# Two-layer mixer and expert-choice MoE on one core: the planner's costs of each step, and a step between engines

## The chip, the core and the metric

One core of a Trainium2 chip. The metric is the device time of one execution in microseconds (us), the median over runs. The core's engines run beside each other, each through its own queue of instructions in order: PE (TensorE, matmuls), DVE (VectorE), ACT (ScalarE), POOL (GpSimd), and SP, whose queue issues the DMA transfers. They wait for one another through semaphores.

## The reference

Two layers work on 256 latent tokens and 256 context tokens of 1024 channels, all in float32. In short:

```python
for l in range(DEPTH):                                   # 2 layers
    u = modulate(rms_norm(h), mod[0], mod[1])            # mod = silu(c) @ ada_w[l] + ada_b[l], six parts
    z = u @ w_in[l]                                      # one projection for four mixers and their gates
    ys = diff_attention(z), hyena(z), conformer(z), latent_attention(z)
    acc = sum(sigmoid(gate[i]) * (ys[i] @ w_branch[l][part i]) for i in range(4))
    h = h + mod[2] * (acc @ w_out[l])
    u = modulate(rms_norm(h), mod[3], mod[4])
    aff = softmax(u @ w_router[l])                       # 16 experts, each takes its top tokens
    h = h + mod[5] * scatter(gate * (silu(hg) * hu) @ w_exp_out[l])   # hg, hu = u[idx] @ w_exp_in[l]
return rms_norm(h)
```

In layer 1 only the latent tokens are finished. The expert weights are the bulk of the bytes: 16 experts of 12 MB in each of the two layers.

## The kernel before

Matmuls are done in three passes (`mm3`, L351): each operand is cut into a high and a low part (`split`, L346: ACT casts the high part at L348, DVE subtracts at L349), and L355, L356 and L357 are the three products. A weight piece of the input projection thus passes DMA (`wi`, L857), ACT, DVE (both into `wq`) and PE (`pm`). PSUM tiles come from small rings: `pm` has 2, `psc` 3, `px` 1, `pt` some.

The program is made of generators: the input projection (`stream`, L832), which feeds the gates (`tg`, L972), hyena, the conformer (`ca` taps on DVE at L1218, its norm at L1230 to L1250), two attentions (scores L1547, maxima L1260 and L1262, exponentials on ACT L1264, transposes L1270, products L1524, the differential norm L1533 to L1536, its end L1505 to L1510), `branch` (L986), which multiplies a mixer's output by a part of `w_branch` (cast to `wbrh` and `wbrl`) and adds the gated result to `acc` (L1042 to L1047), and the output projection (the end of `body`, L956 to L963): a unit of 24 matmuls, then `yo` on DVE (L960), the residual add on POOL (L961), and after it the transposes of `h` (L1742). The generator `products` (L466) makes the modulation vectors on DVE: for each 256 KB `aw` load (L283) a pair of multiplications with a running sum (L510, `aj` and `aw`), 192 instructions in layer 0; when a group is complete, four small instructions follow (L525, L526, L413, L414). The generator `loader` (L1633) issues the loads of expert weights: large `we` of 1 MB (L1678), small ones of 256 KB (L1676), as buffers come free, and the loads of `x` into `h` (L1593). Then the experts run (`experts`, L1936).

What sets the order is a planner, `Order` (L145). It holds a model clock for each engine and one for DMA (`load`: 2.95 us per MB). A generator yields either an event to wait for, a time, or a dictionary of costs by engine; `run` picks the first generator, in order of place, whose time has come on the model's PE clock, lets it emit its instructions, and books the costs: each engine of the dictionary starts when it is free and the engine ahead of it in the dictionary is done. The time that comes out is the earliest for the generator's next step. Since every engine runs its instructions in the order in which they were emitted, the costs set nothing but that order. `_a`, `_d` and `_q` are the costs of an instruction of n columns on ACT, DVE and POOL. Tuned numbers beside them (rings, leads, lags such as `PACE` in `products`) stay.

Of the kernel before, what the change touches and what calls it, by code (L numbers as in the profile page):

```python
# [144 lines left out]
class Order:  # L145
# [29 lines left out]
    def run(self, gens):  # L175

        live = [[g, self.first.pop(g, 0.0), None, None, self.wait.get(i, 0.0)] for i, g in enumerate(gens)]
        place = [i + self.place.get(i, 0) for i in range(len(gens))]
        live = [live[i] for i in sorted(range(len(gens)), key=lambda i: place[i])]
        while live:  # L180
            best = None
            for th in live:
                if th[2] is not None:
                    if th[2].t is None:
                        continue
                    th[1], th[2] = max(th[1], th[2].t), None
                if th[1] - th[4] <= self.t["pe"]:
                    best = th
                    break
                if best is None or th[1] - th[4] < best[1] - best[4]:  # L190
                    best = th
            assert best is not None, [th[0].__name__ for th in live]
            self.t["pe"] = max(self.t["pe"], best[1])
            try:
                y = best[0].send(best[3])
            except StopIteration:
                live.remove(best)
                continue
            best[3] = None
            if isinstance(y, Ev):  # L200
                best[2] = y
            elif isinstance(y, dict):
                e = self.t["pe"]
                for k, c in y.items():
                    k = k.strip()
                    if k == "pe" and e < self.cold:
                        c *= 2
                    e = self.t[k] = max(self.t[k], e) + c
                best[3] = e
            else:  # L210
                best[1] = y


def _a(n):
# [1 line left out]


def _d(n):
    return 0.07 + n / 960


def _q(n):
    return 0.1 + n / 480


@with_exitstack
def kernel(ctx: ExitStack, tc: tile.TileContext, x, ctxt, cols, skip, lamb, fng, ta, tb, tcn, td,
# [169 lines left out]
    def layer(l):  # L397
# [434 lines left out]
        def stream(items):  # L832
# [65 lines left out]
            def body():  # L898
                for j, (src, kind, units, fn, evs) in enumerate(items):
                    for s in range(2) if last else ((0,) if kind == "t" else (0, 1)):  # L900
                        if l == 0 or s == 1 or not last or (kind == "n" and units[0] == 0) or (kind == "t" and units[0] == 0):
                            yield us_ev[s]
                    if kind == "t":
                        t0, tn = units
                        for m in range(2):
                            yield p_ev[j, m]
                            wh, wl = parts[j, m]
                            if fn is gate_out:
                                yield from S.until(lambda: tg_n[0] < TGMAX)
                                tg_n[0] += 1  # L910
                            p = pm()

                            step = 256 if last else tn
                            for c in range(0, tn, step):
                                terms = [(wh[:, k, :], wl[:, k, :], u_at(0, k, t0 + c, step), u_at(1, k, t0 + c, step))
                                         for k in range(KC)]
                                for k in range(0, KC, PIECE[l]):
                                    if k == 4 and l == 0:
                                        yield us_ev[1]
                                    mm3(p[:, c:c + step], terms[k:k + PIECE[l]], first=k == 0, last=k == KC - PIECE[l])  # L920
                                    if c + step < tn or k < KC - PIECE[l]:
                                        yield {"pe": 3 * PIECE[l] * step * 0.00042}
                            done(j, m)
                            cost = fn(p[:, :tn], evs[m])
                            e = yield {"pe": 3 * PIECE[l] * step * 0.00042, **cost}
                            evs[m][0].t = e
                    else:
                        yield p_ev[j, 0]
                        yield p_ev[j, 1]
                        w = 160 if fn is kv_out else 256  # L930
                        for t in units:
                            pv = pm()[:, :w]
                            mm3(pv, [(u_at(0, k, t * 128, 128), u_at(1, k, t * 128, 128), parts[j, k // 4][0][:, k % 4, :w],
                                      parts[j, k // 4][1][:, k % 4, :w]) for k in range(KC)])
                            cost = fn(pv, evs, t)
                            e = yield {"pe": 24 * 0.00042 * w, **cost}
                        evs[0].t = e
                        done(j, 0, 1)

                drop(4)  # L940
                keep()
                gates_done.t = S.t["pe"]
                yield mods[l]["ev"][1]
                if l == 0:
                    yield res_ev
                for k in range(KC):
                    yield acc_ev[k]
                drop(len(accs))
                for q in range(4):
                    for i in range(2):  # L950
                        yield p_ev[jo + q, i]
                    w = [parts[jo + q, i] for i in range(2)]
                    c = slice(q % 2 * 256, q % 2 * 256 + 256)
                    for t in tchunks:
                        p = pm()[:, :256]
                        tt = slice(t * 128 - q0, (t + 1) * 128 - q0)  # L956
                        mm3(p, [(ac[k][0][:, tt], ac[k][1][:, tt], w[k // 4][0][:, k % 4, :], w[k // 4][1][:, k % 4, :])
                                for k in range(KC)])
                        o, hv = t2("yo", w=256), h[t][q // 2][:, c]
                        nc.vector.tensor_tensor(o, p, m2[t // 2][q // 2][:, c], op=OP.mult)  # L960
                        (nc.vector if q == 3 else nc.gpsimd).tensor_tensor(hv, hv, o, op=OP.add)  # L961
                        e = yield {"pe": 24 * 0.108, "dve": _d(256), "dve " if q == 3 else "pool": _d(256)}
                        h_ev[t, q].t = e  # L963
                    del w
                    done(jo + q, 0, 1)
# [20 lines left out]
        def branch(i, os, k0, ready, early):  # L986
# [34 lines left out]
            for d2 in range(4):  # L1021
# [5 lines left out]
                for m in range(2):  # L1027
# [6 lines left out]
                    g = tg.pop((i, kd))  # L1034
                    tg_n[0] -= 1
                    acc_n[kd] += 1
                    PE = {"pe": nk * 3 * TQ * 0.00042, "dve": _d(TQ)}
                    if acc_n[kd] == 1:
                        nc.vector.scalar_tensor_tensor(a, g, 1.0, p[:, :TQ], op0=OP.add, op1=OP.mult)
                        yield PE  # L1040
# [44 lines left out]
        def hyena():  # L1085
# [8 lines left out]
                tabs.append([c.rearrange("p (a f) -> p a f", a=2) for c in hl])  # L1094
                yield {"act": _a(512), "pool": _q(512)}
            cf, sf, ci, si = tabs
            MF = 12 * 0.213 * F

            def to_tokens(c0, name, parts):
                r = []  # L1100
# [1030 lines left out]
```

## Time and profile before

| | us |
|---|---|
| median of 3 runs | 2000.3 (1995.5 to 2003.9) |
| the profiled execution | 2003.7 |
| its span, first to last instruction | 2001.9 |
| PE busy | 1700.4 (85%) |
| DVE busy | 971.6 (49%) |
| ACT, POOL busy | 461.8 (23%), 217.3 (11%) |
| mean granted clock of PE | 0.913 |

The profile is of one execution. Its stages: layer 0's mixers from 0 to about 690 us, its experts to about 1150, layer 1's mixers to about 1535, its experts to the end. A row of a timeline gives the start, the duration, the engine, the line, the operation, output and inputs, the count, and in brackets how long the engine had been idle just before and what ended that. Buffer numbers are left out of names. The granted clock is a share of 2.4 GHz, the mean over the stretch.

### The profile page before, as it was taken

What the parts mean: (1) busy time and instruction counts of PE and PEld (TensorE: products, weight loads), DVE (VectorE), ACT (ScalarE), POOL (GpSimd) and SP (SyncE); (2) the same over time, 40 slices, a digit from 0 to 9 for tenths busy, and PEclk for the clock granted to TensorE, in tenths of its full rate; (3) what the DMA queues carried; (4) which work ended last, traced back from release to release, by engine and by line L of the source; (5) the groups of instructions that cost most, each with busy time, mean ns of one, the idle gap of its engine ahead of it and who ended that gap; (6) DMA issues with size and microseconds to landing.
All of it is one profiled execution on the core that took longest, in us unless ns stands there. A gap on an engine that the chain in (4) does not pass through costs nothing.

```text
span 2001.9 us, 27922 instructions
## 1 busy us (share of the span) xinstructions
PE 1700.4 (85%) x11128; PEld 1108.5 (55%) x11128; DVE 971.6 (49%) x2052; ACT 461.8 (23%) x933; POOL 217.3 (11%) x229
## 2 busy tenths in 40 slices
PE   5998999887999899899899788998988867666665
PEld 2677788665679634333333278888987423322222
DVE  4886789877764312212432285888864111111012
ACT  4423333323332100100110063344442000000000
POOL 1322011021201000000010042410211000000000
PEclk8999999888999899989999998999998877787777
DMA  7443334423345799999999954565759999999997
GB/s 280 168 140 112 127 116 134 147 90 95 99 134 225 250 365 411 418 418 416 415 415 416 401 177 146 165 200 163 227 185 357 414 414 414 413 413 412 414 413 284
DMA packets 204586, 550.72 MB, mean 275 GB/s; under 512 B 14054, under 2 KB 94120, under 8 KB 173992
## 3 DMA queue, kind: packets, MB, share of 16 engines
q1 hardware_dynamic: 204456, 548.94, 72.8%
q8 instruction: 88, 1.44, 0.3%
q14 instruction: 42, 0.34, 0.1%
HBM read 547.83 MB, written 1.05 MB: 274 GB/s over the span
## 4 chain that ended last, share of the span: by engine, by line
PE 48%; DMA 26%; DVE 14%; issue 6%; ACT 5%; POOL 1%; SPq 0%; ACTq 0%; DVEq 0%; POOLq 0%
DMA we<-in_w_ei_dram 14%; PE pm L1951 10%; DMA we<-in_w_eo_dram 7%; PE pm L355 7%; PE pm L357 6%; PE pm L356 6%; PE psc L1976 4%; DVE wq L349 3%; DMA h<-in_w_eo_dram 3%; PE psc L1840 2%; DVE aw L510 2%; PE psc L355 2%; ACT wq L348 1%; PE psc L357 1%; PE psc L356 1%
## 5 line engine op out<-in xcount | busy, mean ns | idle before, releaser
L1951 PE MATMUL pm<-we,xe 128*32 128x256 f32 (+1 forms) x2912 | 406.9, 542 | 96.3 <-DMA we<-in_w_ei_dram 94.4
L1951 PEld LDWEIGHTS pm<-we,xe 128*32 128x32 f32 (+1 forms) x2912 | 136.7, 136 | 343.3 <-issue 185.2
L355 PE MATMUL pm<-uh,wq 128*128 128x256 f32 (+1 forms) x832 | 293.4, 353 | 7.4 <-ACT wq L348 4.8
L356 PE MATMUL pm<-ul,wq 128*128 128x256 f32 (+1 forms) x832 | 283.7, 341 | 2.4 <-DVE ul L754 1.5
L357 PE MATMUL pm<-uh,wq 128*128 128x256 f32 (+1 forms) x832 | 283.2, 340 | 0.0
L1963 DVE SCALAR_TENSOR_TENSOR ea<-ea,pm 128x512 f32<-128x512 f32 (+1 forms) x32 | 17.7, 554 | 426.7 <-ACT ea L1962 426.7
L349 DVE TENSOR_TENSOR wq<-wi,wq 128x1024 fp32r<-128x1024 f32 x131 | 164.1, 1263 | 91.9 <-ACT wq L348 91.5
L1976 PE MATMUL psc<-we,eaT 128*32 128x256 f32 (+1 forms) x1280 | 170.9, 506 | 39.8 <-DMA we<-in_w_eo_dram 37.8
L355 PEld LDWEIGHTS pm<-uh,wq 128*128 128x128 f32 x832 | 161.9, 195 | 29.8 <-ACT wq L348 6.5
L356 PEld LDWEIGHTS pm<-ul,wq 128*128 128x128 f32 x832 | 162.2, 195 | 20.6 <-issue 3.9
L357 PEld LDWEIGHTS pm<-uh,wq 128*128 128x128 f32 x832 | 161.8, 194 | 16.8
L1988 DVE TENSOR_TENSOR ye<-psc,modr 32x512 f32<-32x512 f32 (+1 forms) x120 | 66.4, 553 | 204.8 <-PE psc L1976 203.4
L1976 PEld LDWEIGHTS psc<-we,eaT 128*32 128x32 f32 (+1 forms) x1280 | 58.3, 128 | 146.8 <-issue 74.8
L348 ACT CAST wq<-wi 128x1024 fp32r<-128x1024 f32 x132 | 136.1, 1043 | 10.7 <-DMA wi<-in_w_in_dram 9.3
L1962 ACT ACTIVATE ea<-pm 128x512 f32<-128x512 f32 (+1 forms) x32 | 15.7, 491 | 481.0 <-PE pm L1951 481.0
L1218 DVE SCALAR_TENSOR_TENSOR ca<-up,colt,ca 128x510 f32<-128x510 f32 (+29 forms) x120 | 80.8, 673 | 2.1
L355 PE MATMUL pm<-wq,uh 128*128 128x256 f32 (+1 forms) x240 | 72.7, 303 | 8.1 <-DVE rsq L319 4.0
L2020 ACT COPY eaT<-pt 128x512 f32<-128x512 f32 (+1 forms) x32 | 15.3, 479 | 278.2 <-PE pt L2018 278.2
L510 DVE SCALAR_TENSOR_TENSOR aw<-aw,h 128x512 f32<-128x512 f32 x96 | 77.1, 803 | 3.6
L1264 ACT ACTIVATE e<-psc,nm 128x512 f32<-128x512 f32 (+1 forms) x72 | 44.5, 618 | 146.8 <-DVE nm L1262 144.4
L356 PE MATMUL pm<-wq,uh 128*128 128x256 f32 (+1 forms) x240 | 70.7, 295 | 0.0
L357 PE MATMUL pm<-wq,ul 128*128 128x256 f32 (+1 forms) x240 | 70.7, 295 | 0.0
(407 smaller groups left out, 2639.0 us busy)
## 6 DMA issues: line engine op xcount, KB each, us to landing
we<-in_w_ei_dram SPq DMA_DIRECT2D x233, 1024.0 KB, 13.0
we<-in_w_eo_dram SPq DMA_DIRECT2D x110, 1024.0 KB, 14.6
wi<-in_w_in_dram SPq DMA_DIRECT2D x58, 1024.0 KB, 5.4
aw<-in_ada_t_dram SPq DMA_DIRECT2D x160, 256.0 KB, 5.3
we<-in_w_ei_dram SPq DMA_DIRECT2D x52, 256.0 KB, 9.0
wbr<-in_w_branch_dram SPq DMA_DIRECT2D x40, 256.0 KB, 5.6
h<-in_w_ei_dram SPq DMA_DIRECT2D x40, 256.0 KB, 16.2
h<-in_w_eo_dram SPq DMA_DIRECT2D x40, 256.0 KB, 16.2
```

Of the source, the lines that this page charges most:

```text
L348: nc.scalar.copy(hi, src)
L349: eng.tensor_tensor(lo, src, hi.bitcast(F32), op=OP.subtract)
L355: nc.tensor.matmul(out, lh, rh, start=first and i == 0, stop=False)
L356: nc.tensor.matmul(out, lh, rl, start=False, stop=False)
L357: nc.tensor.matmul(out, ll, rh, start=False, stop=last and i == n - 1)
L510: nc.vector.scalar_tensor_tensor(o, wt_, 1.0, cb[s, k], op0=OP.mult, op1=OP.mult, accum_out=ends[lm, g][0][:, s, c, k:k + 1])
L1218: nc.vector.scalar_tensor_tensor(o, up[:, :, max(d, 0):256 + min(d, 0)], cw[:, c0 + d:c0 + d + 1], o, op0=OP.mult, op1=OP.add)
L1264: nc.scalar.activation(e, p[:, :nk], AF.Exp, scale=scale, bias=nm, accum_out=s)
L1840: nc.tensor.matmul(p[:, kk * n:(kk + 1) * n], h[2 * s + b][k // 4][:, (k % 4) * 128:(k % 4 + 1) * 128], hot[:, 2 * i + b], start=b == 0, s ...
L1951: nc.tensor.matmul(dst[j * M:(j + 1) * M, :], lhs, w[o + j * FW // 512][:, j * FW % 512:j * FW % 512 + FW], start=k == 0, stop=k == KC - 1 ...
L1976: nc.tensor.matmul(py[j * M:(j + 1) * M, :FW], aT[:, c * 128 + q * M:c * 128 + (q + 1) * M], w[f % 2 * 2 + j * FW // 512][:, j * FW % 512: ...
L1988: nc.vector.tensor_tensor(ye[eg][s][c0 // 512][e4 * CAP:(e4 + 1) * CAP, c0 % 512:c0 % 512 + FW], py[r0:r0 + CAP, :FW], mod5[r0:r0 + CAP, c ...
```

## The change

Every engine's step in a dictionary is now followed by a step `HOP` of 0.1 us before the next engine of the same dictionary or the generator's next step may start. The costs of DVE and POOL get a larger fixed part and a larger slope (512 columns on DVE 0.603 to 0.690 us, on POOL 1.17 to 1.29); ACT's stay. A column of a matmul costs 0.000442 us in place of 0.00042 (a unit of 12 matmuls of 512 columns 2.58 to 2.72), a unit of the output projection 24 x 0.119 in place of 24 x 0.108. The number of instructions on PE, DVE, ACT and POOL, their operands and the bytes of the DMA transfers stay; some of the late expert loads go to other buffers. Line numbers of the changed kernel are 4 higher from L213 on.

```diff
@@ class Order, run: one generator's step is booked on the model's clocks
                     if k == "pe" and e < self.cold:
                         c *= 2
                     e = self.t[k] = max(self.t[k], e) + c
+                    e += HOP
                 best[3] = e
...
+HOP = 0.1
...
 def _d(n):
-    return 0.07 + n / 960
+    return 0.13 + n / 915

 def _q(n):
-    return 0.1 + n / 480
+    return 0.15 + n / 450
...
-                                        yield {"pe": 3 * PIECE[l] * step * 0.00042}
+                                        yield {"pe": 3 * PIECE[l] * step * 0.000442}
...
-                            e = yield {"pe": 24 * 0.00042 * w, **cost}
+                            e = yield {"pe": 24 * 0.000442 * w, **cost}
...
-                        e = yield {"pe": 24 * 0.108, "dve": _d(256), "dve " if q == 3 else "pool": _d(256)}
+                        e = yield {"pe": 24 * 0.119, "dve": _d(256), "dve " if q == 3 else "pool": _d(256)}
...
-                    PE = {"pe": nk * 3 * TQ * 0.00042, "dve": _d(TQ)}
+                    PE = {"pe": nk * 3 * TQ * 0.000442, "dve": _d(TQ)}
...
-            MF = 12 * 0.213 * F
+            MF = 12 * 0.226 * F
```

What it does to the order is shown at three places of layer 0. The first is the start of the output projection. On SP, with `wi` for its weights, `we` for the experts' and `aw` for the modulation products, before:

```order
L1593 DMA h_76<-in_x_dram 128x512
L995 DMA wbr<-in_w_branch_dram 128x2x256 x2
L857 DMA wi<-in_w_out_dram 128x8x256 x2
L1678 DMA we<-in_w_ei_dram 128x2048 x5
L1676 DMA we<-in_w_ei_dram 128x512 x4
L1678 DMA we<-in_w_ei_dram 128x2048 x2
L857 DMA wi<-in_w_out_dram 128x8x256
```

and changed:

```order
L287 DMA aw<-in_ada_t_dram 128x512 x3
L861 DMA wi<-in_w_out_dram 128x8x256
L287 DMA aw<-in_ada_t_dram 128x512
L1682 DMA we<-in_w_ei_dram 128x2048 x5
L1680 DMA we<-in_w_ei_dram 128x512 x4
L287 DMA aw<-in_ada_t_dram 128x512 x2
L1597 DMA h_74<-in_x_dram 128x512
L1597 DMA h_75<-in_x_dram 128x512
L1597 DMA h_76<-in_x_dram 128x512
L1682 DMA we<-in_w_ei_dram 128x2048 x2
L861 DMA wi<-in_w_out_dram 128x8x256
```

The `aw` loads and the three loads into `h` stood ahead of the expert loads and now stand among and behind them. On DVE at the same place, before (`acc` and `al` are the end of the gated sum, `yo` is the first work on the projection's results):

```order
L349 TENSOR_TENSOR wq<-wi,wq 128x1024
L1042 SCALAR_TENSOR_TENSOR tg<-tg,psc 128x512
L1047 TENSOR_TENSOR acc<-acc,tg 128x512
L1718 COPY cb_164<-psc 128x32
L349 TENSOR_TENSOR al<-acc,ah 128x512
L960 TENSOR_TENSOR yo<-pm,r_4716 128x256 x2
L1745 COPY hT<-pt 128x256
```

and changed, with one more pair of L514 just ahead of the first row:

```order
L514 SCALAR_TENSOR_TENSOR aj,ad<-aw,h_74 128x512
L514 SCALAR_TENSOR_TENSOR aw,ad<-aw,h_76 128x512
L514 SCALAR_TENSOR_TENSOR aj,ad<-aw,cb 128x512
L514 SCALAR_TENSOR_TENSOR aw,ad<-aw,h_75 128x512
L514 SCALAR_TENSOR_TENSOR aj,ad<-aw,h_74 128x512
L514 SCALAR_TENSOR_TENSOR aw,ad<-aw,h_76 128x512
L529 TENSOR_TENSOR as<-ad 128x32
L530 SCALAR_TENSOR_TENSOR modB_90<-as,colt 128x32
L417 TENSOR_SCALAR modA_89<-modB_90 128x16
L418 TENSOR_TENSOR modA_89<-modA_89,colt 128x16
L964 TENSOR_TENSOR yo<-pm,r_4718 128x256 x2
```

Four pairs of products and the four small instructions of their group now stand ahead of `yo`.

The second place is DVE ahead of the branch matmuls for which PE waits at 381 us. Before, from the split of the last weight piece to `wbrl`:

```order
L349 TENSOR_TENSOR wq<-wi,wq 128x1024
L510 SCALAR_TENSOR_TENSOR aj,ad<-aw,h_74 128x512
L510 SCALAR_TENSOR_TENSOR aw,ad<-aw,h_76 128x512
L1218 SCALAR_TENSOR_TENSOR ca<-up,colt,ca 128x2x243
L1218 SCALAR_TENSOR_TENSOR ca<-up,colt,ca 128x2x242
L1260 TENSOR_REDUCE mx<-psc 128x1
L1262 TENSOR_SCALAR nm<-mx 128x1
L1260 TENSOR_REDUCE mx<-psc 128x1
L1262 TENSOR_SCALAR nm<-mx 128x1
L349 TENSOR_TENSOR wbrl<-wbr,wbrh 128x512
```

and changed, from behind the split and one pair of taps on:

```order
L514 SCALAR_TENSOR_TENSOR aj,ad<-aw,cb 128x512
L514 SCALAR_TENSOR_TENSOR aw,ad<-aw,h_75 128x512
L1416 TENSOR_TENSOR ol<-px,oh 128x128
L1222 SCALAR_TENSOR_TENSOR ca<-up,colt,ca 128x2x244
L1222 SCALAR_TENSOR_TENSOR ca<-up,colt,ca 128x2x243
L514 SCALAR_TENSOR_TENSOR aj,ad<-aw,h_74 128x512
L514 SCALAR_TENSOR_TENSOR aw,ad<-aw,h_76 128x512
L1222 SCALAR_TENSOR_TENSOR ca<-up,colt,ca 128x2x243
L1222 SCALAR_TENSOR_TENSOR ca<-up,colt,ca 128x2x242
L1264 TENSOR_REDUCE mx<-psc 128x1
L1266 TENSOR_SCALAR nm<-mx 128x1
L514 SCALAR_TENSOR_TENSOR aj,ad<-aw,cb 128x512
```

After the last row come the second product of its pair, the second maximum and `wbrl`. Two more pairs of products and two more pairs of taps stand in the stretch, and one pair of products is between the maxima.

The third place is DVE ahead of the branch matmuls for which PE waits at 486 us. Before, from the split on:

```order
L349 TENSOR_TENSOR wq<-wi,wq 128x1024
L1493 RECIPROCAL re<-re 128x2
L1494 TENSOR_SCALAR e<-e,re,lamt 128x512
L1495 SCALAR_TENSOR_TENSOR e<-e,re 128x512
L1510 SCALAR_TENSOR_TENSOR ol<-pt,gsub_100,oh 128x128 x4
L1260 TENSOR_REDUCE mx<-psc 128x1
L1262 TENSOR_SCALAR nm<-mx 128x1
L510 SCALAR_TENSOR_TENSOR aj,ad<-aw,cb 128x512
L510 SCALAR_TENSOR_TENSOR aw,ad<-aw,h_75 128x512
L1260 TENSOR_REDUCE mx<-psc 128x1
L1262 TENSOR_SCALAR nm<-mx 128x1
L349 TENSOR_TENSOR wbrl<-wbr,wbrh 128x512
```

and changed, with a split of `wq` just ahead of the first row:

```order
L1497 RECIPROCAL re<-re 128x2
L1498 TENSOR_SCALAR e<-e,re,lamt 128x512
L1499 SCALAR_TENSOR_TENSOR e<-e,re 128x512
L514 SCALAR_TENSOR_TENSOR aj,ad<-aw,cb 128x512
L514 SCALAR_TENSOR_TENSOR aw,ad<-aw,h_75 128x512
L1537 TENSOR_REDUCE ssd<-do 128x4
L323 TENSOR_SCALAR rsq<-ssd 128x4
L1540 TENSOR_TENSOR do<-px,rsd 128x512
L1264 TENSOR_REDUCE mx<-psc 128x1
L1266 TENSOR_SCALAR nm<-mx 128x1
L1264 TENSOR_REDUCE mx<-psc 128x1
L1266 TENSOR_SCALAR nm<-mx 128x1
```

`wbrl` is next after it. The four `ol` are gone from the stretch, and a norm (`ssd`, `rsq`, `do`, with a power on POOL between the last two) is in. On PE, two units of the input projection now stand between the scores and these branch matmuls, where before there was none.

## Rows read from the trace of the kernel before

**Rows 1.** Windows: us, busy by engine, PEclk (granted clock), DMA share, GB/s.

```profile
381.00:388.00 7.00, 6.68 (x20) 4.87 (x21) 6.52 (x14) 0.64 (x2) 1.27 (x1) 0.53 0.97 313
750.00:1140.00 390.00, 364.34 (x1660) 137.45 (x1658) 104.90 (x188) 32.23 (x62) 6.92 (x9) 0.97 1.02 415
1490.00:1530.00 40.00, 36.07 (x300) 35.22 (x299) 20.63 (x45) 12.49 (x30) 7.72 (x11) 1.00 0.95 351
1540.00:1990.00 450.00, 310.48 (x3310) 133.48 (x3313) 60.85 (x144) 19.34 (x51) 1.28 (x1) 0.77 1.01 405
```

**Rows 2.** Timeline before 381 us: start, us, engine, operation, idle before and its end.

```profile
366.46 1.09 PE L1406 MATMUL px<-aT,mv 128*64 128x128 f32 x16
374.82 1.23 DVE L349 TENSOR_TENSOR wq<-wi,wq 128x1024 fp32r<-128x1024 f32 x1 [0.69 <-ACT wq L348]
377.30 1.48 DVE L1218 SCALAR_TENSOR_TENSOR ca<-up,colt,ca 128x486 f32<-128x486 f32 x2
378.70 0.42 DVE L1260 TENSOR_REDUCE mx<-psc 128x1 f32<-128x256 f32 x1
381.32 0.79 PE L355 MATMUL psc<-oh,wbrh 128*128 128x512 f32 x1 [7.02 <-ACT wbrh L348]
```

**Rows 3.** Timeline of DVE and PE before 426 us.

```profile
418.89 0.19 DVE L525 TENSOR_TENSOR as<-ad 128x32 f32<-128x32 f32 x1
420.73 0.68 DVE L510 SCALAR_TENSOR_TENSOR aj<-aw,h 128x512 f32<-128x512 f32 x1
425.95 0.69 PE L1230 MATMUL pt<-tat,ca 128*128 128x128 f32 x2 [3.97 <-DVE ol L1510]
```

**Rows 4.** Timeline of PE, DVE and ACT before 486 us.

```profile
472.87 1.13 PE L1547 MATMUL psc<-qk 64*128 64x512 f32 x4
476.72 1.22 DVE L349 TENSOR_TENSOR wq<-wi,wq 128x1024 fp32r<-128x1024 f32 x1
485.72 0.61 ACT L348 CAST wbrh<-wbr 128x512 fp32r<-128x512 f32 x1
486.38 0.80 PE L355 MATMUL psc<-oh,wbrh 128*128 128x512 f32 x1 [12.38 <-ACT wbrh L348]
```

**Rows 5.** Waits of PE, 180 to 700 us: us in total, times, longest.

```profile
PE psc L355 <- ACT e L1264: 5.7, 3, 3.3
PE pt L1505 <- DVE cx L1249: 1.2, 1, 1.2
```

**Rows 6.** DMA issues: count, KB each, median us to landing; 605:640, then whole run.

```profile
we<-in_w_ei_dram SPq DMA_DIRECT2D x4, 256.0 KB, 12.2
aw<-in_ada_t_dram SPq DMA_DIRECT2D x160, 256.0 KB, 5.3
```

**Rows 7.** Timeline at the output projection of layer 0.

```profile
616.88 1.92 SPq L1676 DMA_DIRECT2D we<-in_w_ei_dram  x4
622.39 0.42 DVE L960 TENSOR_TENSOR yo<-pm,r 128x256 f32<-128x256 f32 x1 [1.81 <-PE pm L357]
622.90 0.74 POOL L961 TENSOR_TENSOR h<-h,yo 128x256 f32<-128x256 f32 x1 [29.97 <-DVE yo L960]
625.07 0.38 PE L1742 MATMUL pt<-tat,h 128*128 128x128 f32 x2
```

**Rows 8.** Timeline at the end of layer 1's mixers: DVE, PE, SP.

```profile
1482.39 0.41 DVE L1042 SCALAR_TENSOR_TENSOR tg<-tg,psc 128x256 f32<-128x256 f32 x1
1483.87 0.43 DVE L349 TENSOR_TENSOR ahl<-acc,ahl 128x256 fp32r<-128x256 f32 x1 [0.53 <-ACT ahl L348]
1484.21 0.41 DVE L1042 SCALAR_TENSOR_TENSOR tg<-tg,psc 128x256 f32<-128x256 f32 x1
1501.17 0.39 PE L355 MATMUL pm<-wq,ahl 128*128 128x256 f32 x1 [1.66 <-ACT ahl L348]
1489.51 10.66 SPq L1678 DMA_DIRECT2D we<-in_w_ei_dram  x5
1502.57 22.82 SPq L1678 DMA_DIRECT2D we<-in_w_ei_dram  x7
```

More of the change, by code (lines that the diff above doesn't have):

```diff
@@ L921, in body @@
                                     if c + step < tn or k < KC - PIECE[l]:
-                                        yield {"pe": 3 * PIECE[l] * step * 0.00042}
+                                        yield {"pe": 3 * PIECE[l] * step * 0.000442}
                             done(j, m)
                             cost = fn(p[:, :tn], evs[m])
-                            e = yield {"pe": 3 * PIECE[l] * step * 0.00042, **cost}
+                            e = yield {"pe": 3 * PIECE[l] * step * 0.000442, **cost}
                             evs[m][0].t = e
```

## The prediction

> **What bounds the kernel now.** I read the windows by stage first, then the gaps of TensorE (PE) and what ended them, then the timelines of VectorE (DVE), ScalarE (ACT) and the DMA queue around the longest gaps. In layer 0's experts the DMA engines are full from 750 to 1140 us (share 1.02, 415 GB/s), in layer 1's from about 1490 (0.95, then 1.01) [rows 1]. So the end is the time at which expert weights may start to flow in a layer, plus bytes over a fixed rate; and they may start when buffers come free at the end of the mixers, where PE is the busy engine. The change issues the same matmuls and the same bytes, so its worth is the sum of PE gaps in the two mixer stages. Three long gaps stand in layer 0: 7.02 us ended at 381.32, 3.97 at 425.95, 12.38 at 486.38, each ended by ACT or DVE work [rows 2 to 4]. After the first, PE's granted clock was 0.53 for 7 us [rows 1]: 1.2 GHz most of that time, so that gap cost about 7 x 0.47 = 3.3 us more.
>
> **What the change is.** Costs set only the order. A step is now 0.1 us later on each engine after the first, and DVE and GpSimd (POOL) steps cost more (512 columns on DVE 0.603 -> 0.690 us). The chains through DVE and ACT therefore ripen later in the model, while PE work without a chain (the input projection) is pulled ahead; the modulation products (L510, a pair per 256 KB `aw` load, about 1.4 us a pair) fall behind: where the output projection of layer 0 begins, before has emitted all of them 30 us of PE work earlier, and the change still has four pairs to go.
>
> **First gap, 381 us: worse.** Before: from the start of the `wq` split at 374.82 come the split and a pair to 377.30 (2.48), two `ca` taps to 378.70 (1.40), then maxima, exponentials and the cast of `wbrh` to PE at 381.32 (2.62): 6.5 us [rows 2]. In the changed order three tap pairs and three product pairs stand in that stretch, one pair between the two maxima, ahead of the exponential that ACT does before the cast: 2.48 + 2 x 1.36 + 3 x 1.40 + 2.62 = 12.0, that is 5.5 more. (A product took 0.68 [rows 3], so a pair 1.36.) Against it, PE has a px block (1.09 [rows 2]) and four transposes left for that time, some 1.5 us. **+4**, between +2 (if DVE gets ahead by a pair) and +5.5. Queued behind it on ACT is nothing that another gap needs.
>
> **Second gap, 426 us: better.** Before, four small instructions that finish a modulation group run from 418.89 to 420.73 ahead of the pair and the `ol` chain that PE waits for at 425.95 [rows 3]. The change has them 43 us of PE work later: 1.8 us off a gap of 3.97, and a shorter gap may keep the clock: **-2.5**, between 0 and -5. The gap after it, which `cn` ends, stays: the pair that stood between the maxima now stands behind them, but still ahead of `cn`.
>
> **Third gap, 486 us: better.** Before, no input projection is left between the last score matmul (done at 474.0) and the branch unit; the split starts at 476.72, the cast of `wbrh` at 485.72, PE at 486.38: 9.7 us from the split [rows 4]. In the change the chain from the split keeps its exponentials, one pair and two maxima; the four `ol` are gone and a norm with a trip to POOL is in, and I put one against the other. But two input-projection units stand on PE ahead of the branch unit, 2.7 us each by the kernel's constants, and some 2.2 us of transposes and scores (the last of these took 1.13 [rows 4]); the split can start about 1.7 us after the unit before them, a tanh and a cast on ACT later. 1.7 + 9.7 - 7.6 = 3.8, and up to 2 more if DVE comes in late: 4 to 6 instead of 12.4. **-7**, between -8.5 and -4. Two short gaps lose what is ahead of them and go: one before `cx` (1.2) and the shortest of three that wait for `e` (5.7 together, the longest 3.3) [rows 5]: **-2**. The longer two of these have as much ahead of them in either order: 0, give or take 2.
>
> **New: the output projection of layer 0.** Before, the DMA queue issues `wi`, five 1 MB `we`, and then four 256 KB `we` from 616.88 [rows 7]; those four took a median 12.2 us to land, with the five ahead of them [rows 6]. In the change the last two `aw` loads stand directly behind the four. Issued at about 619, with the same 12.2, they land at 631 to 632. DVE runs in order: after the last `al` split stand four product pairs, four small instructions (0.2 each, as the one at 418.89 [rows 3]), and only then the first `yo`, which before ran at 622.39 [rows 7]. The first two pairs have their data; the last two start at about 631.5. 631.5 + 2 x 1.36 + 0.8 + `yo` 0.42 + POOL's add 0.74 + hops 0.2 = 636.3. PE does two units of the projection and at 625.07 [rows 7] comes to the transpose of `h`, which needs that add, and both `pm` buffers are full: it waits until 636.3, **11.2 us**. Queued behind on the DMA queue are three `h` loads (wanted 6 us later) and two `we`; the fourth `wi` waits for `yo` anyway. If the loads landed as an `aw` does over the whole run (median 5.3 [rows 6]), at 624.3, the same chain would end at 629.1: 4.0 us. So 4 to 11.2; I take 11.2, since the rows nearest to it are the four small loads in that very queue. After a gap of that length the clock falls as after the first: 2 us more (0 to 3.3). **+13.**
>
> The Trainium skill (page DMA: Bandwidth & Descriptors, section Queues, rings and completion order) says that within a queue descriptors are taken in order on each DMA engine, but that completion is not first in, first out: a later load may be done before an earlier one. By that rule the small loads could overtake megabytes. Here the trace speaks against it: 12.2 us behind five large loads, 5.3 alone.
>
> **Layer 1: about +3.** The change emits the end of the input projection 9.5 us of PE work earlier and leaves the last summand of the gated sum for the end: eight branch units in a row. Each needs DVE `tg`, `acc`, a cast on ACT, and `ahl`, before the next `tg`: 1482.39 to 1484.21, 1.8 us, 0.53 of it waiting for the cast [rows 8]. Eight units and three weight splits (0.6 each) make 16; PE has 8 x 0.7 = 5.5 us of its own there, and 2.5 of the projection that needs only the finished sums: +8, less the 1.66 us gap before the last sum [rows 8], which is the same chain, and 1 for what the queue of three `psc` buffers hides: **+5**. The `we` loads, which before start at 1489.51 [rows 8], start earlier by up to 9 us, but the next seven (1502.57) still hang on the projection, and the queue is only about 3 us behind there: -3. Together +5 - 3 + 1 (0 to +3 for the conformer's norm, now last on the chain) = **+3**, between -4 and +8.
>
> **Layer 0 before 345 us**: the same units, some moved by up to 20 us of PE work; PE is 95% busy there from 180 us. 0, give or take 3.
>
> **Sum.** +4 - 2.5 - 7 - 2 + 13 + 3 = **+8.5 us**. The profiled execution took 2003.7 (span 2001.9, 1.8 around it), so 2012; it was 3.4 above the median of the runs, 2000.3. On the median: **2009 us**.
>
> **Rivals.**
> A, faster: DVE is never late and the two `aw` loads overtake the large ones. The wait in the output projection is 4 with no clock loss (-9 against the sum), the first gap grows by 2 only (-2), the third goes to 4 (-1.5), layer 1 comes out at -1 (-4). 2009 - 16.5 = 1992. For it: the two largest old gaps do lose work. Against it: the landing order of the trace. It decides on whether `aw` is there before 627 us.
> B, clearly slower: everything in layer 0 as summed, but the chain of eight units in layer 1 is paid in full and the early loads bring nothing, since their successors hang on the projection: layer 1 +8, and the first gap +5.5, clock loss +1.5: 2009 + 8 = 2017; with gaps at the later layer-0 units (each of which has a product pair in its chain in the change) up to 2023. It decides when the DMA share falls between the early `we` and the projection.
> C, it does not do what it says: the order differs but gaps only change place, within 2 us: 2000. For it: the sum of DVE and PE work is the same.
>
> **How the numbers follow.** Forecast (2003 to 2015) 0.45, A (1988 to 1999) 0.17, B (2015 to 2025) 0.26, C 0.12. A measurement of this kernel tells about 0.5%, 10 us, from no change: 1990.3 to 2010.3 is the same. Of the forecast half lies above 2010.3; of A a third is below 1990.3. Faster 0.07, raised to 0.10 for what the order of two queues does not tell; slower 0.22 + 0.26 = 0.48, lowered to 0.46; same 0.44. Leaving out the lower half of A and the top of B, the range is 1991 to 2022.
>
> **What would show it.** After's trace: a PE gap of about 11 us in the output projection of layer 0, ended by POOL's add or by `yo`, with the last products right ahead of it on DVE and waiting for `aw`; gaps of some 11, 2 and 4 to 6 us where 7, 4 and 12.4 stood; in layer 1 a run of gaps ended by ACT's `ahl` cast before the projection; the DMA-bound stages as long as before, only shifted. The forecast is wrong if `aw` lands before 627 us, or if the DMA stages give back a shift, that is, if they end at the old time after starting late.

## The result and the profile after

The changed kernel took 2014.1 us (median of 9 runs, 2007.7 to 2016.9), the kernel before 2000.8 beside it (9 runs): ratio 1.0057, 95% interval 1.0044 to 1.0070. It is slower by 13 us in the medians, which by themselves would give 1.0067. The profiled execution took 2012.9 (span 2011.1), 9.2 more than that of before, and all differences below are between profiled executions.

The trace is cut here at five instants that each kernel has: the first matmul of layer 0's output projection, its first expert matmul, layer 1's first input projection, layer 1's first matmul of the output projection, its first expert matmul. Each column is the time between two of them in us, the sixth the time from the last of them to the end; the kernels with e1 to e12 are the experiments below.

| kernel | to projection 0 | projection 0 | experts 0 | mixers 1 | projection 1 | experts 1 | span |
|---|---|---|---|---|---|---|---|
| before | 619.2 | 73.9 | 467.6 | 336.1 | 45.4 | 459.7 | 2001.9 |
| after | 610.1 | 91.2 | 470.2 | 336.7 | 44.5 | 458.3 | 2011.1 |
| e1 loads first | 614.0 | 82.2 | 470.1 | 337.8 | 43.9 | 458.0 | 2006.1 |
| e2 products at old cost | 605.0 | 75.3 | 469.7 | 335.3 | 44.5 | 456.1 | 1986.0 |
| e3 new costs in layer 0 | 609.5 | 91.4 | 468.5 | 344.8 | 43.3 | 459.6 | 2017.1 |
| e4 new costs in layer 1 | 618.5 | 73.9 | 468.6 | 356.5 | 44.5 | 458.3 | 2020.4 |
| e5 after, later reads | 615.8 | 91.3 | 468.2 | 332.3 | 44.1 | 459.2 | 2011.0 |
| e6 e4, later reads | 620.1 | 73.9 | 467.6 | 345.0 | 43.8 | 458.8 | 2009.1 |
| e7 e2, later reads | 610.5 | 75.3 | 468.0 | 335.6 | 43.3 | 459.1 | 1991.8 |
| e8 products earlier | 639.3 | 73.5 | 468.0 | 336.2 | 44.2 | 456.2 | 2017.4 |
| e9 before, products later | 608.8 | 91.8 | 466.9 | 336.9 | 45.3 | 457.0 | 2006.6 |
| e10 VectorE costs only | 605.3 | 95.0 | 468.3 | 336.8 | 43.7 | 457.9 | 2006.9 |
| e11 TensorE costs only | 615.4 | 73.6 | 467.2 | 331.1 | 45.7 | 457.0 | 1989.9 |
| e12 step only | 605.3 | 74.2 | 468.3 | 337.6 | 43.6 | 455.5 | 1984.5 |

Kernels with the same order up to the projection differ in the first column between executions: after, e1, e3 and e5 by 6.3 us, before, e4 and e6 by 1.6, e2 and e7 by 5.5. The second column repeats within 0.2. The change wins about 7 to 9 us ahead of the projection (mean of its four 612.4, of the three with the old order 619.3), loses 17.3 in it, and the four other columns sum to +0.9. Of what it wins, 4.7 us are idle time of PE ahead of the projection (71.1 to 73.2 in the four, 76.7 to 77.8 in the three). The rest is PE's busy time, which differs with the granted clock between executions of one order: 536.6 us at 0.96 in e3, 544.7 at 0.94 in e5.

The PE gaps that answer to [rows 2, 3, 4], a new one at 553, and the one in the projection, in the timeline of after (start, us, engine, line, operation, and in brackets the idle time before and what ended it):

```profile
381.26 0.80 PE L359 MATMUL psc<-oh,wbrh 128*128 128x512 f32 x1 [5.73 <-ACT wbrh L352]
423.50 0.33 PE L1234 MATMUL pt<-tat,ca 128*128 128x128 f32 x1 [3.06 <-DVE ol L1514]
465.78 0.79 PE L359 MATMUL psc<-oh,wbrh 128*128 128x512 f32 x1 [7.57 <-ACT wbrh L352]
553.41 0.45 PE L1509 MATMUL pt<-tat,do 128*128 128x128 f32 x1 [6.15 <-DVE do L1540]
631.23 0.47 PE L1746 MATMUL pt<-tat,h 128*128 128x128 f32 x1 [13.44 <-POOL h L965]
```

The last is the hold. Its timeline on SP, DVE and POOL, answering to [rows 7]:

```profile
606.72 2.81 SPq L1682 DMA_DIRECT2D we<-in_w_ei_dram  x5
609.63 2.52 SPq L1680 DMA_DIRECT2D we<-in_w_ei_dram  x4
615.03 2.83 SPq L287 DMA_DIRECT2D aw<-in_ada_t_dram  x2
...
626.38 0.69 DVE L514 SCALAR_TENSOR_TENSOR aj<-aw,cb 128x512 f32<-128x512 f32 x1 [9.21 <-DMA aw<-in_ada_t_dram]
629.95 0.75 DVE L964 TENSOR_TENSOR yo<-pm,r 128x256 f32<-128x256 f32 x2
630.45 1.41 POOL L965 TENSOR_TENSOR h<-h,yo 128x256 f32<-128x256 f32 x2 [47.82 <-DVE yo L964]
```

DVE is idle for 9.21 us at the head of its queue, waiting for one 256 KB load behind nine reads of expert weights; behind it stand the last products, then `yo`, then POOL's add, then PE. The windows of the same 77 us, before and then after (PE busy, other engines, granted clock, DMA share, GB/s):

```profile
613.00:690.00 77.00, 68.16 (x538) 65.93 (x537) 33.35 (x89) 16.23 (x45) 11.08 (x16) 0.92 0.68 245
```

```profile
613.00:690.00 77.00, 57.53 (x461) 56.40 (x461) 29.95 (x84) 14.06 (x42) 11.02 (x16) 0.85 0.54 193
```

PE is busy 10.6 us less and its granted clock falls from 0.92 to 0.85 (of 2.4 GHz; a mean between the two levels).

### The profile page after: what moved, and what is told of

The parts are those of the page before. It is cut to its first block, busy times and chain, and to the rows that moved or that the text cites. A ratio compares the mean times of both kernels' runs of the same rounds, so it can differ in the third digit from the quotient of the medians.

```text
span 2011.1 us, 27928 instructions
## 1 busy us (share of the span) xinstructions
PE 1701.1 (85%) x11128; PEld 1106.2 (55%) x11128; DVE 977.5 (49%) x2052; ACT 463.9 (23%) x933; POOL 221.5 (11%) x229
## 5 line engine op out<-in xcount | busy, mean ns | idle before, releaser
L1955 PE MATMUL pm<-we,xe 128*32 128x256 f32 (+1 forms) x2832 | 402.7, 550 | 92.9 <-DMA we<-in_w_ei_dram 90.6
L359 PE MATMUL pm<-uh,wq 128*128 128x256 f32 (+1 forms) x832 | 290.2, 349 | 10.2 <-ACT wq L352 4.8
L361 PE MATMUL pm<-uh,wq 128*128 128x256 f32 (+1 forms) x832 | 280.5, 337 | 0.0
L1980 PE MATMUL psc<-we,eaT 128*32 128x256 f32 (+1 forms) x1360 | 176.0, 499 | 43.2 <-DMA we<-in_w_eo_dram 41.1
L514 DVE SCALAR_TENSOR_TENSOR aw<-aw,h 128x512 f32<-128x512 f32 x96 | 77.8, 810 | 3.5
L1268 ACT ACTIVATE e<-psc,nm 128x512 f32<-128x512 f32 (+1 forms) x72 | 44.5, 618 | 151.3 <-DVE nm L1266 150.8
```

The lines of the kernel that those rows point to most:

```text
L359: nc.tensor.matmul(out, lh, rh, start=first and i == 0, stop=False)
L361: nc.tensor.matmul(out, ll, rh, start=False, stop=last and i == n - 1)
L514: nc.vector.scalar_tensor_tensor(o, wt_, 1.0, cb[s, k], op0=OP.mult, op1=OP.mult, accum_out=ends[lm, g][0][:, s, c, k:k + 1])
L1268: nc.scalar.activation(e, p[:, :nk], AF.Exp, scale=scale, bias=nm, accum_out=s)
L1955: nc.tensor.matmul(dst[j * M:(j + 1) * M, :], lhs, w[o + j * FW // 512][:, j * FW % 512:j * FW % 512 + FW], start=k == 0, stop=k == KC - 1 ...
L1980: nc.tensor.matmul(py[j * M:(j + 1) * M, :FW], aT[:, c * 128 + q * M:c * 128 + (q + 1) * M], w[f % 2 * 2 + j * FW // 512][:, j * FW % 512: ...
```

## The experiments

### e1, e2: the hold, undone in two ways

e1 leaves every compute engine's order as in the change and only issues layer 0's last two product loads ahead of the nine expert reads:

```diff
+                    if i < len(jobs) and i not in seen:
+                        seen.add(i)
...
                     load(i + AHEAD)
+                    if l == 0 and i == len(jobs) - 5:
+                        load(i + 3)
+                        load(i + 4)
```

> The changed kernel with the last two `aw` loads of layer 0 issued ahead of the five `we` in place of behind the nine; on PE, DVE, ACT and POOL every instruction stands where it stood. Theory (the loads make the hold): the two loads land before the first pairs are done, the last two pairs run right behind them, DVE reaches `yo` about 9 us earlier, the PE gap at the transposes of `h` falls from 13.4 to about 4 us, and the execution is 9 to 12 us shorter than the changed kernel's (about 2003). Rival (four pairs, 5.5 us, ahead of `yo` make it, or buffers do): the gap stays above 9 us and the time within 4 us of the changed kernel's, about 2012.

2006.9 us (ratio to before 1.0018, 1.0002 to 1.0033). The timeline at the projection:

```profile
610.18 2.53 SPq L287 DMA_DIRECT2D aw<-in_ada_t_dram  x3
612.77 2.56 SPq L1686 DMA_DIRECT2D we<-in_w_ei_dram  x5
...
625.81 0.47 PE L1750 MATMUL pt<-tat,h 128*128 128x128 f32 x1 [4.14 <-POOL h L969]
```

The gap falls from 13.44 to 4.14, the stage from 91.2 to 82.2, the median by 7, which is less than the 9 to 12 that I expected. What is left of the hold is DVE's own: four pairs of products still stand ahead of `yo`, and they now run without a wait for data from 618.27 on.

e2 puts the products' steps alone back to their old cost and takes the step off them:

```diff
-                    e = yield {"dve": len(ss) * (_d(512) + 0.07)}
-                    yield e + PACE[l]
+                    e = yield {"dve": len(ss) * (0.07 + 512 / 960 + 0.07)}
+                    yield e + PACE[l] - HOP
```

> The changed kernel, but the steps of the products generator are booked at the old cost and without the step between engines, so that they are emitted earlier and are over before the output projection of layer 0. Theory (their lag is what costs): no PE gap over 3 us at the transposes of `h`, the gaps that have a pair in their chain between 340 and 500 us come out between those of before and those of the change, total about 1998 to 2003. Rival (the other costs reorder the mixers for the worse whatever the products do): 2008 or more.

1993.9 us (0.9958, 0.9938 to 0.9979): faster than before, by more than expected. The last product starts at 598.5, 6.5 us ahead of the projection, no product load stands behind the expert reads, and the stage takes 75.3. All other new costs stayed, so together they are worth having; the price of a product is not.

### e3, e4: one layer at a time

A flag set by the model's own PE clock switches all new costs off (e3) or on (e4) at 1100 us:

```diff
...
+            LATE = self.t["pe"] > 1100.0
...
+                    e += HOP if LATE != True else 0.0      # e3; e4 has False, and so for each cost
```

> The new costs and the step between engines only while the model's PE clock is below 1100 us, the old ones after that: layer 0 is emitted as in the changed kernel, layer 1 nearly as before. The trace of the changed kernel has its whole loss by the first matmul of layer 1 (10.8 us later than before) and gains 1.6 from there. Theory: about 2011 to 2013, that is 10 to 13 us above before. Rival (the loss is spread over both layers): 2004 to 2008.

> The old costs while the model's PE clock is below 1100 us, the new ones and the step after that: layer 0 as before, layer 1 nearly as in the changed kernel. Theory: layer 1 comes out even, the gaps of its branch units ended by `wbrh` and by sums (8 us) against five shorter ones earlier that go: 1997 to 2002. The prediction's term was 3 us slower: 2004. Rival: over 2006.

e3 took 2023.0 (1.0104, 1.0080 to 1.0128), e4 2021.3 (1.0083, 1.0065 to 1.0100): both slower than the whole change and above what I expected. e3's first two columns are the change's, as expected, and its mixers of layer 1 took 8.7 us more than those of before; e4's took 20.4 more. Both traces have one new gap late in layer 1's mixers. Of e4, PE, ACT and SP:

```profile
1482.70 10.03 SPq L1685 DMA_DIRECT2D we<-in_w_ei_dram  x5
1492.83 1.87 SPq L1683 DMA_DIRECT2D we<-in_w_ei_dram  x4
1494.79 3.81 SPq L1002 DMA_DIRECT2D wbr<-in_w_branch_dram  x3
1505.28 0.62 ACT L355 CAST wbrh<-wbr 128x512 fp32r<-128x512 f32 x1 [9.28 <-DMA wbr<-in_w_branch_dram]
1505.95 0.58 PE L362 MATMUL psc<-ohl,wbrh 128*128 128x256 f32 x1 [10.08 <-ACT wbrh L355]
```

It is the hold once more with other names: the last three 256 KB loads of the Conformer's branch weights (branch 2) behind the same nine issues of expert weights. The program lets those reads start when branch 0 has issued its last load (`br_ev`, L1030 in the changed kernel), the last in its list of branches; here branch 2 comes last, and nothing holds the reads back for it. In before the last branch loads were issued from 1474.11 to 1478.69, ahead of the first large read at 1489.51 [rows 8]. In e3 the three loads stand behind the nine as well (1490.74), and the gap is 11.78, though its costs in layer 1 are the old ones: the order of layer 1 also hangs on where layer 0 leaves the model. So neither kernel is one layer of the change alone.

### e5, e6, e7: the branch loads ahead of the reads

The reads wait for all four branches, in layer 1 only:

```diff
+        late = set()
...
-                if i == 0 and d2 == 2:
-                    br_ev.t = 0.0
+                if d2 == 2:
+                    late.add(i)
+                    if i == 0 and not last or last and len(late) == 4:
+                        br_ev.t = 0.0
```

> The change, with one edit in layer 1: the six expert reads of 1 MB that stand ahead of the Conformer branch's last three loads of 0.25 MB in SP's queue may be issued only once all four branches have issued their last load (before, the edit waits for branch 0 alone, and the new order runs branch 0 ahead of branch 2). In the change the last branch casts on ACT wait 4.9 us for those loads and PE's gaps there that name a branch cast are 4.4, then 2.0. Theory (a load behind large reads in one queue is paid in full where PE has no other work): ACT's DMA wait is gone, PE's gap of 2.0 and the small ones with it, 2 to 4 us under the change: 2010 to 2012. Rival (the expert reads that then start later leave the first expert product waiting): the gain comes back at the expert block, 2014 or more.

> The kernel with the old costs until the model's TensorE passes 1100 us and the new ones after, which took 2021 where 1997 to 2002 was expected, now with the same edit as e5. Its trace had one gap of 10.1 us in layer 1, on a branch cast that waited 9.3 us for a load behind six expert reads of 1 MB. Theory: that place in the queue is what layer 1 lost: the gap falls to 1 or 2 us and the time to 2010 to 2013. Rival (layer 1 loses by the new order of its mixers as a whole, and the gap only takes the place of smaller ones): 2018 or more.

> The change with the steps of the modulation products at the old cost (e2, 1993.9 us), now with the edit of e5 as well. e2's trace shows the branch cast waiting 2.5 us for a load behind the six reads and gaps of about 1 us at each of the branch's last products. Theory: 2 to 4 us under e2, 1990 to 1992. Rival (later expert reads cost what is won): 1994 or more.

e6, which is e4 with the edit, took 2010.9 (1.0043, 1.0022 to 1.0065): 10.4 under e4, and the gap of 10.08 is gone. In its timeline the three loads go first:

```profile
1484.72 3.94 SPq L1003 DMA_DIRECT2D wbr<-in_w_branch_dram  x3
1488.72 3.05 SPq L1688 DMA_DIRECT2D we<-in_w_ei_dram  x5
...
1499.31 0.58 PE L362 MATMUL psc<-ohl,wbrh 128*128 128x256 f32 x1 [1.04 <-ACT wbrh L355]
```

So the place in the queue explains the miss in e4 by some 11 of its 20 us. The other 9 (345.0 against 336.1) are not longer gaps: those of 0.5 us and more add up to 22.3 in e6 and 23.3 in before, while PE is busy 8 us longer at a granted clock of 0.93 instead of 0.96. Why the clock was lower there stays open.

e5 took 2012.2 (1.0062, 1.0040 to 1.0084), 2 under the change and not told apart from it by the intervals; its mixers of layer 1 took 332.3 instead of 336.7. e7 took 1993.6 (0.9970, 0.9958 to 0.9983), the same as e2: the 2 to 4 us did not come. Its mixers of layer 1 took 335.6 where e2's took 335.3, and the experts after them 459.1 where e2's took 456.1, as the rival had it, though those of before took 459.7 as well. PE's gaps of 0.5 us and more between 1455 and 1512 sum to 9.9 in the change and 6.9 in e5, to 10.6 in e2 and 10.4 in e7: in e2, whose ACT waited 2.5 us for a load, the place had cost PE nothing that the edit could give back. A place behind large reads costs what PE has nothing to put against.

### e8, e9: the products moved, the costs left

e8 has all new costs, e5's edit, and products that are due earlier in layer 0; e9 is the kernel before, with none of the change, and products that are due later:

```diff
-    PACE, AHEAD = (0.0, -1.5), 2
+    PACE, AHEAD = (-1.5, -1.5), 2     # e8, on the change
+    PACE, AHEAD = (0.6, -1.5), 2      # e9, on the kernel before
```

> The change with all its new costs, the products' steps included, but in layer 0 each product step's next one is due 1.5 us earlier, which ends the products 284 TensorE instructions ahead of the output projection; with the edit of e5. Theory (of the change's costs in layer 0 the one that counts is that the products end too late and their loads come to stand behind the nine expert reads): no gap over 3 us at the transposes behind the first block of the output projection, so 13 less there and 3 less by the edit, against the change's 2014: 1996 to 2001. Rival (earlier products take VectorE from the mixers, and gaps in 350 to 560 grow by what the hold gives): 2006 to 2012.

> The kernel before with nothing of the change, but in layer 0 each product step's next one is due 0.6 us later (128 steps, two at a time), so that the last four product loads come to stand behind the first five expert reads in SP's queue (two do in the change, none before). Theory (the hold at the output projection is made by that place in the queue alone, whatever moved the products): a gap at the transposes behind the projection's first block of at least the change's 13.4, the stage from the projection's first product to the first expert product 91 to 97 us instead of 73.9, and 2014 to 2022. Rival (the hold needs the new order of the mixers before it): the stage stays at 74 to 78, 1998 to 2004.

e9 took 2009.3 (1.0039, 1.0022 to 1.0056), between the range of the theory and that of the rival. Its projection stage is 91.8, like the change's, with four product loads behind the reads:

```profile
608.15 1.98 SPq L1676 DMA_DIRECT2D we<-in_w_ei_dram  x4
611.13 8.34 SPq L283 DMA_DIRECT2D aw<-in_ada_t_dram  x4
...
623.50 0.69 DVE L510 SCALAR_TENSOR_TENSOR aj<-aw,cb 128x512 f32<-128x512 f32 x1 [9.02 <-DMA aw<-in_ada_t_dram]
631.04 0.48 PE L1742 MATMUL pt<-tat,h 128*128 128x128 f32 x1 [14.60 <-POOL h L961]
```

That shows the hold without the change. It shows something else that I had not expected: the way to the projection is 608.8 instead of 619.2. Later products leave DVE to the mixers' chains (192 products belong to this stage; by 480 us e9 has done 132, before 148), and PE's gaps of 0.5 us and more from 180 to 605 us sum to 28.9 instead of 42.3. So a delay of the products by itself gives at least as much ahead of the projection as the change won there, and costs as much in it.

e8 took 2017.2 (1.0085, 1.0063 to 1.0108): the rival's way, and above even its range. The hold is gone (73.5), but the projection starts at 639.3. Two windows, e8 and then after:

```profile
480.00:620.00 140.00, 114.01 (x509) 89.65 (x508) 95.43 (x193) 46.98 (x89) 20.71 (x18) 0.88 0.30 99
```

```profile
480.00:620.00 140.00, 119.62 (x585) 95.99 (x583) 104.83 (x224) 44.23 (x80) 20.10 (x21) 0.95 0.43 148
```

Gaps from 180 to 605 us sum to 53.7 (after 38.8), and the granted clock is 0.88 instead of 0.95. Up to the projection PE idles 86.3 us where it idled 73.2 in after, and is busy 553.0 where it was 536.9.

### e10, e11, e12: one third of the change each

```diff
 # e10: HOP = 0.0 and TensorE's old constants;   e11: HOP = 0.0 and the old _d, _q
 # e12: the old _d, _q and TensorE's old constants, and only
+                    e += HOP
```

> Of the change only the costs of VectorE and GpSimd, without the step between engines and with TensorE's old constants. In its order four product loads stand behind the expert reads. Theory: the products are steps of VectorE alone, so a higher cost there delays them against everything else and this part by itself makes the hold: the projection's stage 91 to 97 us, 2012 to 2022. Rival (four loads behind five reads cost no more than in the kernel before because the products need them later): below 2004.

> Of the change only TensorE's three constants (5 to 10% up). In its order the products end 236 TensorE instructions ahead of the output projection (36 in e2, 284 in e8, none in the change), with no product load behind the expert reads. Theory from e8 (products that run early take VectorE from the mixers, and the time to the projection grows by more than the hold costs): no hold, the projection's stage 73 to 76 us, but its first product at 630 to 640 us, 2010 to 2020. Rival (e8 lost for another reason and early products are free): first product at 605 to 620, 1990 to 2000.

> Of the change only the step of 0.1 us between engines, all constants as before. In its order the products end 12 TensorE instructions ahead of the projection and no product load stands behind the expert reads; in layer 1 one branch load stands behind them. Theory (what e2 won over the kernel before, 11 us ahead of the projection, comes from the step, which counts each hand-over in the mixers' chains): first projection product at 606 to 612, 1990 to 1997. Rival (it comes from the constants): 617 to 621, 1999 to 2004.

e10 took 2009.9 (1.0038, 1.0026 to 1.0051), e11 1992.0 (0.9947, 0.9929 to 0.9965), e12 1987.4 (0.9928, 0.9911 to 0.9946).

VectorE's costs (with GpSimd's) make the hold alone, and with four product loads behind the reads a longer one; the time came out 2 under what I expected:

```profile
630.26 0.47 PE L1746 MATMUL pt<-tat,h 128*128 128x128 f32 x1 [18.65 <-POOL h L965]
```

TensorE's costs alone pull the products forward (the last starts at 566.8, against 583.6 in before and 628.5 in after) and give 615.4 and no hold. My expectation from e8, that early products cost 20 us, fell: in e8 the last is no earlier (574.0), so the products' time alone did not make e8 slow. What did is not settled.

The step alone is the best of all, 3 us under what I expected: the last product starts at 604.6, just ahead of the projection at 605.3, with no product load behind the reads. The waits of PE from 180 to 700 us, before and then e12 (us in total, times, longest):

```profile
PE psc L355 <- ACT wbrh L348: 21.9, 3, 12.4
PE psc L355 <- ACT e L1264: 5.7, 3, 3.3
```

```profile
PE psc L359 <- ACT wbrh L352: 10.7, 2, 6.7
PE psc L359 <- ACT e L1268: 3.1, 4, 0.9
```

It still waits in layer 1, where one branch load stands behind the reads:

```profile
1468.69 1.97 SPq L1680 DMA_DIRECT2D we<-in_w_ei_dram  x4
1470.71 0.44 SPq L999 DMA_DIRECT2D wbr<-in_w_branch_dram  x1
1481.61 0.62 ACT L352 CAST wbrh<-wbr 128x512 fp32r<-128x512 f32 x1 [9.29 <-DMA wbr<-in_w_branch_dram]
1482.28 0.58 PE L359 MATMUL psc<-ohl,wbrh 128*128 128x256 f32 x1 [10.52 <-ACT wbrh L352]
```

e12 with the edit of e5 was not tried; by e6, where a gap of 10.1 went with 10.4 us, it might come to some 1977, an estimate; e7, where the same edit won nothing, had no such gap.

## Why the prediction was right, and where its steps were not

The time and its cause were right: the hold in the output projection, made by two product loads behind the expert reads, outweighs what the mixers win. That the sum came so near is in part luck, as the terms show:

- **Output projection, +13: it was +17.3.** Mechanism as told, link by link. The chain from the first product on the landed load to PE's transpose took 4.85 us (626.38 to 631.23) where I had 4.8. What was mis-sized is the landing: I had the two loads there 12.3 us after the projection's first matmul (631.5 less 619.24), and it was 16.2 and 16.9 (626.35 and 626.99 less 610.10). I had taken the reads' times from before, where one of the five large ones was issued 9.4 us ahead of that matmul and the other four from 4.5 ahead; in after all five were issued from 3.4 ahead, so more bytes were still in front of the two loads. They were not issued as the projection begins either, but 4.9 and 7.4 us after it (the last section says why). A row of before that I had not used shows the same for the two loads behind its four small reads, issued at 619.66 and 622.16:

```profile
619.66 2.82 SPq L1678 DMA_DIRECT2D we<-in_w_ei_dram  x2
```

The late issue did not make the landing later, as far as the rows tell: the first three of the small reads ahead landed at 623.70, 624.35 and 625.02, and the two loads followed behind the fourth at that pace. PE's wait began 7.7 us into the projection (I had 5.8) and ended at 21.1 (I had 17.1). The gap was 13.44 instead of 11.2, another of 1.03 came with it, and of the 2.8 that are left 2.3 are PE's busy time in the stage, 66.8 us at a granted clock of 0.83 instead of 64.5 at 0.91. By the Trainium skill's rule (page DMA: Bandwidth & Descriptors, section Queues, rings and completion order) the small loads might have been done first; the traces do not bear that out: the first of them landed at 626.35 in after, 1505.20 in e4, 623.48 in e9 and 622.70 in e10, each behind the last of the reads ahead whose landing is recorded (625.02, 1504.44, 622.80, 622.02). Rival A, which rested on it, did not come.
- **First gap, +4: it was -1.3**, with the clock behind it 0.76 where it was 0.53 [rows 1]. The window of after behind the gap, and the split ahead of it in DVE's timeline:

```profile
381.00:388.00 7.00, 6.74 (x27) 5.17 (x28) 6.59 (x14) 0.72 (x3) 1.29 (x1) 0.76 0.36 122
```

```profile
369.34 1.23 DVE L353 TENSOR_TENSOR wq<-wi,wq 128x1024 fp32r<-128x1024 f32 x1 [0.60 <-ACT wq L352]
```

The chain from this split to PE took 11.9 us (369.34 to 381.26), and I had 12.0. But before PE ran out 0.5 us ahead of the split [rows 2], and I let it run out 1 us behind; in the change it ran out 6.2 us behind the split's start (381.26 less 5.73, less 369.34). I had asked what DVE does after the split and not what moves the split. In after PE also waited just ahead of this gap, where before it did not: 1.31 us ended at 369.85, and 2.63 ended at 373.57 by an `ol` that stood behind taps and products on DVE. With these the stretch has 9.7 us of gaps where before had 7.0: the +4 was nearer than the one gap says.
- **Second gap, -2.5: it was -0.9**, and the gap behind it that `cn` ends, 3.4 in before, which I left standing, is gone.
- **Third gap, -7: it was -4.8.** From the split to PE there were 9.65 us (456.13 to 465.78), and I had 9.7. PE's own work after the split covered 2.1 of them, not the 5.9 that I had: the split had waited 2.1 for ACT.
- **Two short gaps, -2:** the one before `cx` went, and the three waits for `e` fell from 5.7 to 1.8 together, more than I had. But 6.15 at 553.41 and 4.22 at 559.57 came, both with products ahead in DVE's chain, where before had 2.53 at 569.11: +7.8 that I had put into rival B. The sum ahead of the projection, -7.5, was met by -9.1 (or -6.9 by the means), and that is luck: errors cancel, and PE's idle time up to the projection fell by 3.5 alone (76.7 to 73.2), while 5.7 of the 9.1 are busy time at a granted clock of 0.96 instead of 0.94, which the terms hardly counted.
- **Layer 1, +3: it was 0** (336.7 + 44.5 against 336.1 + 45.4). The run of branch units at the end is there, but its price was paid elsewhere: the early expert reads, which I booked at -3, came ahead of branch loads, and ACT waited 4.91 us for one. By e5's trace they cost 4 in that stage instead of winning 3; its time does not confirm it.

The larger thing that I missed is not in the time. I costed the change as one; e12 shows that its step alone makes the kernel 0.7% faster, and e10 that VectorE's costs alone make the hold.

## What to carry to other kernels

When costs set the order, a truer cost can still move one chain past a point that the planner doesn't price, here small loads that come to stand behind megabytes in one in-order queue; look up each queue's order at such points before the time. Change such constants one kind at a time: two of the three parts won 10 and 14 us alone, the third lost 8, and together they lost 13. A gate that names the unit which happens to be last (branch 0) is true only for the order that it was written under: let it count all of them.

## What the runs showed of the hardware

In all fourteen traces the loads that SP issued landed in the order of their issue, as far as their landings are recorded (some 650 in each), and small ones behind large ones took longer: 256 KB took 11.3 and 9.5 us from issue to landing in after, and a median of 2.8 in e1, where they were issued ahead of the reads.

SP's issues also waited for landings. The waits of SP's queue in after, 604 to 632 us (us in total, times, longest):

```profile
SPq L287 <- DMA we<-in_w_ei_dram: 4.9, 2, 2.8
```

With the nine expert reads issued, the two `aw` issues began at 615.03 and 617.53, and the second and third of the large reads had landed at 614.97 and 617.47; in e9 four issues came at 611.13, 614.19, 616.66 and 619.15, behind landings at 611.12, 614.13, 616.60 and 619.09. This is not the chip but the program. Its loads on SP use eight semaphores in turn to tell of their landing, and ahead of an issue SP waits for the semaphore's last use: in all fourteen traces every load has the semaphore of the one eight places ahead, and none was issued before that one's recorded landing. So at most eight loads of SP are under way, which sets when a load is issued. Here the landing followed from the bytes ahead instead: from the first large read's issue to the first product load's landing 19.6 us in after (606.72 to 626.35) and 22.4 in e9 (601.06 to 623.48).
